# A gated linear-attention layer: value unit moved to the end of a head, steps at fixed places, two copies moved to ScalarE

## The chip, the cores and the metric

The kernel runs on one core of one Trainium2 chip. The metric is the device time of one execution in microseconds (us). One profiled execution gives the trace; the runs that are timed without a profile give the median.

## The reference, cut to what matters

One layer over 512 latent and 256 context tokens of width 2048. Two groups work on the same normalised input: a gated recurrence (RG-LRU, called A here) and a linear attention with a decay per key channel (HGRN2, called B here), 16 heads of 128 channels, run in both directions. The change touches B alone:

```
f = lb + (1 - lb) * sigmoid(f_pre);  k = 1 - f;  q = silu(q_pre)      # for each direction
S_t = diag(f_t) S_{t-1} + k_t v_t^T;  o_t = q_t S_t                   # 16 heads, chunked, forward and backward
y  = rmsnorm(o_fwd + o_bwd) * silu(g);  x = x + gate * (concat(y_A, y_B) @ w_out);  out = rmsnorm(x)
```

`gate` comes from `silu(c) @ ada_w`, a vector product that the kernel sums on VectorE ("gate sums").

## The kernel before, in words

**Tiling.** The projection is a list of units. A unit is 128 output columns of w_in: 16 blocks of 128 rows, in four groups g = 0..3 of four blocks k. Each block is three matmuls (the weights are split into a high and a low part, `whi` and `wlo`, and so is the input). A unit that needs only latent tokens (q, gb) has matmuls of 512 columns; one that needs all tokens (ff, fb, v) has pairs of 256 and 512 columns. Before each group, `p_conv` makes one `whi` (a cast on ScalarE) and one `wlo` (a subtraction on GpSimd) for a group four ahead, and `p_dma` fetches a weight tile on SP's queue six ahead. When a unit's last group is through, `evac_b` takes the unit's result out of PSUM.

**A head of B** is five units: q, gb (output gate), ff and fb (decay gates forward and backward) and v. From `ff` and `fb`, `evac_b` makes T (the decay f) and KK (k = 1 - f) with a sigmoid on ScalarE and two operations on VectorE. Then come the steps of the head, all of whose matmuls are put between the projection's matmuls on TensorE, in program order:

- `prep`: kd = k forward + k backward, the two halves of QQ = q * f (VectorE), and Kc, a copy of k (ScalarE);
- `level(0)` to `level(6)`: 16 (or 8) small score matmuls, then KK, QQ and T are multiplied or paired up for the next level (VectorE); level 0 begins with the diagonal `diag`, which needs kd, and then needs Kc and both halves of QQ; level 5 copies blocks of `mc` into `mg`;
- `ktr` x4 and, for v, x4: transposes of KK and v on VectorE, 16 instructions each;
- `umm` x3: state matmuls from the two transposed tiles; `omm`: 12 output matmuls of 128 x 128, then on ScalarE four squares, a table load and a square root, on VectorE a reciprocal and four scalings; `otr`: 16 transposes on VectorE; `fin`: one product (`ys`) and its store on GpSimd's queue.

**Order of the steps before.** A queue `wq`. After every second block TensorE's program comes to a place where `run_steps(1)` may take a step from the queue's head: at k = 3 always, at k = 1 only if the step is marked `fast` (transposes). The units of a head stand in the order q, gb, ff, v, fb, so the steps of a head are queued when its fb is out, and run beside the next head's units.

**Gate sums before.** In heads 1 to 13, at g = 2 of every unit, `gate_step` adds one weight tile (fetched by `gate_raw` in the unit before, from the same ring of six tiles as the weights) to `gacc` with one VectorE instruction.

**Engines are in order.** Each engine runs its instructions in program order; one that waits holds all behind it.

**Where a place stands.** 40 places to a head, two to a group. In the changed kernel place n of head h is reached after the n-th pair of blocks counted from the head's q. In a q or gb unit a place is six matmuls of 512 columns, in the others six pairs.

Of the kernel before, what the change touches and what calls it, by code (L numbers as in the profile page):

```python
# [8 lines left out]
F32 = mybir.dt.float32  # L9
F32R = mybir.dt.float32r  # L10
U8 = mybir.dt.uint8
AF = mybir.ActivationFunctionType
# [23 lines left out]
START = [0, 16, 1, 17, 18]  # L36
NS = len(START)
ORDER_A = [2] + [cb for h in range(3, NH) for cb in (16 + h, h)]
ORDER_B = [32 + g * 16 + h for h in range(NH) for g in (0, 4, 1, 3, 2)]


def view(t, off, dims):
# [9 lines left out]
def layer_kernel(ctx: ExitStack, tc, xT, xres, w0, wi, adas, adag, adagb, wo, par, lw, fw, cst, masks, out):  # L52
# [449 lines left out]
    evac_ga(2, PG[2])  # L502
    wq.append(lb1)

    gst = {}

    def gate_raw(i):
# [4 lines left out]
    def gate_step(i):  # L512
        q, kb = divmod(i, KB)
        if q >= 4:
            return
        if kb == 0:
            gst["acc"] = bw.tile([128, 512], F32, name="gacc", bufs=2)
        a = gst["acc"]
        t = wlin(gst.pop(("raw", i)))
        if kb == 0:  # L520
            dve.tensor_scalar(a, t, sc[:, 0:1], None, op0=ALU.mult)
        else:
            dve.scalar_tensor_tensor(a, t, sc[:, kb:kb + 1], a, op0=ALU.mult, op1=ALU.add)
        gate_raw(i + 1)
        if kb == KB - 1:
            def go():
                b = bq.tile([1, 512], F32, name="sg")
                sp.dma_start(b, adagb[q:q + 1, :])
                ph = psw.tile([128, 512], F32, name="w")
                pe.matmul(ph, ones, a, start=True, stop=True)  # L530
                o = ystage.tile([1, 512], F32, name="ys")
                dve.tensor_add(o, ph[0:1, :], b)
                pool.dma_start(gate_d[q:q + 1, :], o)
            wq.insert(1, go)

    bw = None
    bst = {}
# [2 lines left out]
        act.activation(dst[:, 0:C], ph[:, 0, 0:C], AF.Sigmoid)  # L540
        act.activation(dst[:, C:TA], ph[:, 1, :], AF.Sigmoid)

    def fast(f):
        f.fast = True
        return f

    def transpose(dst, src, ks):
        for i in ks:
            for j in range(4):
                dve.transpose(dst[32 * j:32 * j + 32, :, 32 * i:32 * i + 32], src[32 * i:32 * i + 32, :, 32 * j:32 * j + 32])  # L550

    def evac_b(h, kind, ph):
        s = bst.setdefault(h, {})
        if kind in ("q", "gb"):
            sg = bq.tile([128, T], F32, name="sg")
            act.activation(sg, ph[:, 1, :], AF.Sigmoid)
            t = bq.tile([128, T], F32, name=kind, bufs=2)
            dve.tensor_mul(t, ph[:, 1, :], sg)
            s[kind] = t
        elif kind == "v":  # L560
            t = bw.tile([128, TA], F32, name="ktok")
            act.copy(t[:, 0:C], ph[:, 0, 0:C])
            act.copy(t[:, C:TA], ph[:, 1, :])  # L563
            vt = bw.tile([128, 6, 128], F32, name="vtok", bufs=2)
            s["v"] = vt

            for i in range(4):
                wq.append(fast(lambda i=i: transpose(vt, t.rearrange("p (a b) -> p a b", b=128), (i,))))
        else:
            d = 0 if kind == "ff" else 1  # L570
            if d == 0:
                s["T"] = bw.tile([128, 2, TA], F32, name="T0")
                s["K"] = bw.tile([128, 2, TA], F32, name="KK")
            f, k = s["T"][:, d, :], s["K"][:, d, :]
            sig2(f, ph)
            i = 16 * d + h
            dve.tensor_scalar(f, f, lbt[:, 1, i:i + 1], lbt[:, 0, i:i + 1], op0=ALU.mult, op1=ALU.add)
            dve.tensor_scalar(k, f, -1.0, 1.0, op0=ALU.mult, op1=ALU.add)
            if d == 1:
                wq.extend(steps_b(h))  # L580

    def steps_b(h):
        s = bst[h]
# [32 lines left out]
        def level(l):  # L616
            def go():
                m = 1 << l
                if l == 0:
                    diag()  # L620
                K, Q, Tm = s["K"], s["Q"], s["T"]
                pw = psw.tile([128, 512], F32, name="w")
                if l < 5:
                    tiles32(pw, lambda c, j: s["Kc"][:, c, 32 * j:32 * j + 32],
                            lambda c, j: view(Q, 128 * c + 32 * j, [[2 * m, 16 // m], [T + m, 2], [1, m]]))
                elif l == 5:
                    tiles32(pw, lambda c, j: K[:, j % 2, C + 128 * c + 32 * j:C + 128 * c + 32 * j + 32],
                            lambda c, j: Q[:, 1 - j % 2, 128 * c + 32 * (j ^ 1):128 * c + 32 * (j ^ 1) + 32])
                else:
                    for c in range(4):  # L630
                        for j in range(2):
                            k0, q0 = C + 128 * c + 64 * j, 128 * c + 64 * (1 - j)
                            pe.matmul(pw[64 * j:64 * j + 64, 64 * c:64 * c + 64], K[:, j, k0:k0 + 64],  # L633
                                      Q[:, 1 - j, q0:q0 + 64], start=True, stop=True)
                nb = TA // m
                kk = view(K, 0, [[2 * m, nb // 2], [TA + m, 2], [1, m]])
                dve.tensor_mul(kk, kk, view(Tm, 1, [[2, nb // 2], [nb - 1, 2], [0, m]]))  # L637
                if l < 4:
                    kc_copy(2 * m)
                qq = view(Q, 0, [[2 * m, C // m], [T + m, 2], [1, m]])  # L640
                dve.tensor_mul(qq, qq, view(Tm, nb + 1 + C // m, [[2, C // m], [-nb - 1, 2], [0, m]]))  # L641
                T2 = bw.tile([128, 2, nb // 2], F32, name=f"T{l + 1}")
                dve.tensor_mul(T2.rearrange("p a b -> p (a b)"), view(Tm, 0, [[2, nb]]), view(Tm, 1, [[2, nb]]))  # L643
                s["T"] = T2
                if l < 5:
                    dve.copy_predicated(s["mc"], MK[:, l, None, :].to_broadcast([128, 4, 32]),
                                        pw[:, 0:128].rearrange("p (a b) -> p a b", b=32))
                elif l == 5:
                    mg = bw.tile([128, 4, 128], F32, name="mg")
                    s["mg"] = mg  # L650
                    for j in range(4):
                        r = slice(32 * j, 32 * j + 32)
                        i = j ^ 1
                        act.copy(mg[r, :, 32 * i:32 * i + 32], pw[r, 0:128].rearrange("p (a b) -> p a b", b=32))
                        dve.tensor_copy(mg[r, :, r], s["mc"][r])  # L655
                else:
                    p4 = pw[:, 0:256].rearrange("p (a b) -> p a b", b=64)
                    act.copy(s["mg"][0:64, :, 64:128], p4[0:64])
                    dve.tensor_copy(s["mg"][64:128, :, 0:64], p4[64:128])
            return go  # L660
# [53 lines left out]
            pool.dma_start(y_d[KB + h], y)  # L714
            del bst[h]

        return ([prep] + [level(l) for l in range(7)] + [fast(ktr(i)) for i in range(4)] + [umm(0), umm(4), umm(8), omm, otr, fin])

    def run_steps(n):
        for _ in range(n):  # L720
# [28 lines left out]
    for i in range(NP):  # L749
# [21 lines left out]
        for k in range(4):  # L771
            mm_unit(ph if full else ph[:, 1, :], hi[:, k, :], lo[:, k, :], 4 * g + k, full)
            if k % 2 == 0:
                continue
            if grp == "A":
                credit += 1.5 if full else 1.0
                while credit >= 1.33:
                    credit -= 1.33
                    run_steps(1)
            elif u < NA + 3:  # L780
                left = 2 * (4 * NA + 10 - i) + (k == 1)
                run_steps(max(1, -(-len(wq) // max(1, left))))
            elif k == 3 or (wq and hasattr(wq[0], "fast")):
                run_steps(1)
        if grp == "A":
            if g == 3:
                if cb >= 16:
                    evac_ga(cb - 16, ph[:, 1, :])
                else:
                    evac_xa(cb, ph[:, 0, 0:C], ph[:, 1, :])  # L790
                    push_a(cb)
        elif u >= NA + 5 and g == 2 and gi < 4 * KB:
            if gi == 0:
                gate_raw(0)
            gate_step(gi)
            gi += 1
        elif g == 3:
            evac_b(cb % 16, kind, ph)

    hctx.close()  # L800
# [39 lines left out]
    for q in range(4):  # L840
# [13 lines left out]
        for kb in range(2 * KB):  # L854
# [3 lines left out]
            if q == 0:  # L858
                y_conv(kb + 2)
                y_dma(kb + 4)  # L860
                if wq:
                    run_steps(1)
                elif op is None:
                    rctx.close()
                    qctx.close()
                    rctx = ExitStack()
                    yp2 = rctx.enter_context(tc.tile_pool(name="yp2", bufs=1, side="right"))
                    op = rctx.enter_context(tc.tile_pool(name="op", bufs=1, side="right"))
                    ssq = op.tile([128, 4, 4], F32, name="ssq")
# [85 lines left out]
```

## Time and profile before

| what | value |
|---|---|
| median of 3 runs (lowest, highest) | 2327.13 us (2324.47, 2329.04) |
| the profiled execution's own time | 2325.76 us |
| its span, first to last instruction | 2323.9 us |
| TensorE matmul busy | 2241.1 us (96%) |
| VectorE, GpSimd, ScalarE busy | 1424.9 (61%), 934.7 (40%), 883.8 us (38%) |
| mean granted TensorE clock | 0.996 of full speed |

Busy time of TensorE counts matmuls whose ends are modelled, so a short wait behind a matmul shows a little shorter in it than from start to start.

### The profile page before, as it was taken

To read this page: it belongs to the slowest core of one execution; us is meant where nothing else is said; L and a number is where in the kernel's file an instruction comes from. 1 tells how busy PE (TensorE), PEld (TensorE's weight loads), DVE (VectorE), ACT (ScalarE), POOL (GpSimd) and SP (SyncE) were. 2 spreads that over 40 slices of the span, in tenths; PEclk is the share of its full clock that TensorE was granted. 3 is DMA by queue.
4 is the path that set the end of the run, shared out by engine and by line. 5 is a ranking of instruction groups with operands and counts; after the bars stand their busy time and mean duration, and the time that the engine had idled before them with its cause. 6 is when DMAs were issued, how large, how long until landed. Compare 5 with 4: busy or idle time off the path is not lost.

```text
span 2323.9 us, 38899 instructions
## 1 busy us (share of the span) xinstructions
PE 2241.1 (96%) x15520; PEld 1867.6 (80%) x15520; DVE 1424.9 (61%) x2223; ACT 883.8 (38%) x1605; POOL 934.7 (40%) x682
## 2 busy tenths in 40 slices
PE   5999999999999999999999999999999998999998
PEld 3778888888888788888888878878878887788886
DVE  5557666666667766775786786686676577710011
ACT  4247776777622232232232223223223233332222
POOL 1235555565533333433343333333333233355552
PEclk9999999999999999999999999999999999999999
DMA  8952222222222222222222222222222123553433
GB/s 323 345 188 78 82 82 82 82 91 78 74 78 82 82 84 83 81 92 73 74 94 79 76 90 83 73 91 78 87 79 76 61 65 114 159 173 96 126 122 109
DMA packets 119086, 241.95 MB, mean 104 GB/s; under 512 B 13556, under 2 KB 13940, under 8 KB 118904
## 3 DMA queue, kind: packets, MB, share of 16 engines
q1 hardware_dynamic: 116216, 231.06, 30.1%
q0 software_dynamic: 2688, 8.40, 0.9%
q8 instruction: 122, 2.00, 0.3%
q14 instruction: 60, 0.49, 0.1%
HBM read 226.81 MB, written 12.59 MB: 103 GB/s over the span
## 4 chain that ended last, share of the span: by engine, by line
PE 65%; DVE 21%; issue 5%; ACT 5%; DMA 2%; POOL 2%; SPq 0%; ACTq 0%; POOLq 0%; DVEq 0%
PE m L180 23%; PE m L179 12%; PE w L850 8%; PE m L182 8%; PE m L850 6%; DVE ktok L550 5%; DVE KK L637 4%; DVE QQ L641 3%; PE w L678 2%; PE w L372 2%; DVE T L643 1%; DMA araw<-in_adas 1%; PE w L182 1%; POOL i L385 1%; DVE mg L655 1%
## 5 line engine op out<-in xcount | busy, mean ns | idle before, releaser
L128 POOL TENSOR_TENSOR wlo<-wraw,whi 128x512 fp32r<-128x512 f32 x556 | 786.5, 1419 | 1123.5 <-ACT whi L127 1054.6
L180 PE MATMUL m<-h,whi 128*128 128x512 f32 x1984 | 737.5, 394 | 0.0
L179 PE MATMUL m<-h,whi 128*128 128x256 f32 x1984 | 562.9, 284 | 1.4 <-ACT xp L323 1.4
L127 ACT CAST whi<-wraw 128x512 fp32r<-128x512 f32 x556 | 342.5, 620 | 548.8 <-PE m L180 181.0
L182 PE MATMUL m<-h,whi 128*128 128x512 f32 x1440 | 455.9, 398 | 0.0
L180 PEld LDWEIGHTS m<-h,whi 128*128 128x128 f32 x1984 | 372.0, 188 | 81.6 <-issue 0.7
L180 PE MATMUL m<-h,wlo 128*128 128x512 f32 x992 | 390.4, 394 | 0.0
L179 PEld LDWEIGHTS m<-h,whi 128*128 128x128 f32 x1984 | 374.7, 189 | 4.2 <-ACT xp L323 1.9
L182 PEld LDWEIGHTS m<-h,whi 128*128 128x128 f32 x1440 | 263.4, 188 | 54.8 <-issue 0.5
L182 PE MATMUL m<-h,wlo 128*128 128x512 f32 x720 | 281.2, 391 | 0.0
L179 PE MATMUL m<-h,wlo 128*128 128x256 f32 x992 | 278.9, 281 | 0.0
L180 PEld LDWEIGHTS m<-h,wlo 128*128 128x128 f32 x992 | 185.9, 187 | 44.6
L179 PEld LDWEIGHTS m<-h,wlo 128*128 128x128 f32 x992 | 187.4, 189 | 0.0
L637 DVE TENSOR_TENSOR KK<-KK,T 128x768 f32<-128x768 f32 x112 | 176.5, 1576 | 3.0 <-PE w L633 1.8
L182 PEld LDWEIGHTS m<-h,wlo 128*128 128x128 f32 x720 | 135.2, 188 | 29.6
L340 DVE SCALAR_TENSOR_TENSOR u<-xp,P,u 128x256 f32<-128x256 f32 x96 | 88.1, 978 | 104.1 <-ACT u L338 104.1
L550 DVE STREAM_TRANSPOSE ktok<-KK 32x384 f32<-32x384 f32 x256 | 145.7, 569 | 3.3
L587 ACT COPY Kc<-KK 128x512 f32<-128x512 f32 x80 | 54.7, 684 | 176.1 <-DVE KK L637 120.0
L641 DVE TENSOR_TENSOR QQ<-QQ,T 128x512 f32<-128x512 f32 x112 | 115.5, 1031 | 0.4
L550 DVE STREAM_TRANSPOSE vtok<-ktok 32x192 f32<-32x192 f32 x256 | 94.6, 369 | 13.2 <-ACT ktok L563 10.0
L850 PE MATMUL m<-whi,yh 128*128 128x512 f32 x256 | 102.1, 399 | 0.0
L850 PE MATMUL m<-wlo,yh 128*128 128x512 f32 x256 | 101.2, 395 | 0.0
(209 smaller groups left out, 3075.9 us busy)
## 6 DMA issues: line engine op xcount, KB each, us to landing
wraw<-in_wi SPq DMA_DIRECT2D x428, 256.0 KB, 3.1
araw<-in_adas SPq DMA_DIRECT2D x64, 512.0 KB, 8.8
wraw<-in_wo SPq DMA_DIRECT2D x128, 256.0 KB, 2.6
wraw<-in_adag SPq DMA_DIRECT2D x64, 256.0 KB, 2.6
y_d<-ys POOLq DMA_DIRECT2D x32, 256.0 KB, 2.4
wraw<-y_d SPq DMA_DIRECT2D x32, 256.0 KB, 2.8
h<-in_xT SPq DMA_DIRECT2D x16, 384.0 KB, 7.6
w0raw<-in_w SPq DMA_DIRECT2D x16, 320.0 KB, 9.6
```

The lines of the kernel that those rows point to most:

```text
L127: act.copy(hi, t)
L128: pool.tensor_sub(lo, t, hi.bitcast(F32))
L179: pe.matmul(ph[:, 0, 0:C], w, h[:, 0:C], start=s, stop=e)
L180: pe.matmul(ph[:, 1, :], w, h[:, C:TA], start=s, stop=e)
L182: pe.matmul(ph, w, h[:, C:TA], start=s, stop=e)
L340: dve.scalar_tensor_tensor(dst, xp[:, o + k:o + k + n], cw, dst, op0=ALU.mult, op1=ALU.add)
L372: pe.matmul(pl, w[:, i, :], x[:, C:TA], start=n == 0, stop=n == 2)
L550: dve.transpose(dst[32 * j:32 * j + 32, :, 32 * i:32 * i + 32], src[32 * i:32 * i + 32, :, 32 * j:32 * j + 32])
L587: act.copy(kc.rearrange("p c n -> p (c n)").rearrange("p (a b c) -> p a b c", b=2, c=m), view(s["K"], C, [[2 * m, C // m], [TA + m, 2], [1 ...
L637: dve.tensor_mul(kk, kk, view(Tm, 1, [[2, nb // 2], [nb - 1, 2], [0, m]]))
L641: dve.tensor_mul(qq, qq, view(Tm, nb + 1 + C // m, [[2, C // m], [-nb - 1, 2], [0, m]]))
L850: pe.matmul(pos[tk], y[:, 128 * tk:128 * tk + 128], wlin(x), start=(kb == 0 and n == 0), stop=(kb == 2 * KB - 1 and n == 2))
```

## The change

The units of a head now stand as q, gb, ff, fb, v. The queue for B's steps is gone: every step has a fixed place, counted from its own head's q: prep 33, levels 34, 37, 39, 42, 45, 48, 51, the KK transposes 52, 54, 56, 57, those of v 58 to 61, umm 62, 64, 66, omm 68, otr 69, fin 71 (places from 40 on lie beside the next head; places after 56 of the last head are spread by 1.9). k = 1 - f is an ACTIVATE (Identity) on ScalarE, and so are level 5's four copies of `mc`. v's staging tile has its own buffer. The five gate tiles of a head are fetched after ff's last group, fb's first three and v's first, and each is added one group later.

```diff
-ORDER_B = [32 + g * 16 + h for h in range(NH) for g in (0, 4, 1, 3, 2)]
+ORDER_B = [32 + g * 16 + h for h in range(NH) for g in (0, 4, 1, 2, 3)]
...
+    def at(slot, f):
+        sched.setdefault(slot, []).append(f)
...
-        gate_raw(i + 1)
...
-            wq.insert(1, go)
+            at(slot_now + 5, go)
...
+    PREP, LEVEL = 33, (34, 37, 39, 42, 45, 48, 51)
+    KTR, VTR, UMM, OMM, OTR, FIN = (52, 54, 56, 57), (58, 59, 60, 61), (62, 64, 66), 68, 69, 71
+    GATES = {("ff", 3), ("fb", 0), ("fb", 1), ("fb", 2), ("v", 0)}
+    def put(h, slot, f):
+        s = 2 * 20 * h + slot
+        if h == NH - 1 and slot > 56:
+            s += (slot - 56) * 9 // 10
+        at(s, f)
...
-            t = bw.tile([128, TA], F32, name="ktok")
+            t = bw.tile([128, TA], F32, name="vraw")
...
-            dve.tensor_scalar(k, f, -1.0, 1.0, op0=ALU.mult, op1=ALU.add)
+            act.activation(k, f, AF.Identity, scale=-1.0, bias=ones[:, 0:1])
...
-                        dve.tensor_copy(mg[r, :, r], s["mc"][r])
+                        act.copy(mg[r, :, r], s["mc"][r])
...
-            elif k == 3 or (wq and hasattr(wq[0], "fast")):
-                run_steps(1)
+            run_slot(slot_now)
...
-        elif u >= NA + 5 and g == 2 and gi < 4 * KB:
-            if gi == 0:
-                gate_raw(0)
+        if ("raw", gi) in gst:
             gate_step(gi)
             gi += 1
-        elif g == 3:
+        if u >= NA + 5 and (kind, g) in GATES:
+            gate_raw(gi)
+        if g == 3:
             evac_b(cb % 16, kind, ph)
```

In the output projection that follows the units, each weight block kb now runs the two places that are its own, before its matmuls.

VectorE's program before, from one head's `omm` (the reciprocal) to the next head's `prep` (kd and the two QQ), in the middle of B:

```order
L701 RECIPROCAL ss<-ss 128x4
L703 TENSOR_SCALAR kd<-w,ss 128x128 x4
L550 STREAM_TRANSPOSE mg<-kd 32x4x32 x16
L523 SCALAR_TENSOR_TENSOR gacc<-wraw,sc,gacc 128x512
L712 SCALAR_TENSOR_TENSOR ys<-mg,P,gb 128x512
L550 STREAM_TRANSPOSE vtok<-ktok 32x6x32 x16
L523 SCALAR_TENSOR_TENSOR gacc<-wraw,sc,gacc 128x512
L577 TENSOR_SCALAR T_7457<-T_7457,lbt 128x768
L578 TENSOR_SCALAR KK<-T_7457 128x768
L595 TENSOR_TENSOR kd<-KK 128x512
L598 TENSOR_TENSOR QQ<-q,T_7457 128x512
L599 TENSOR_TENSOR QQ<-q,T_7457 128x512
```

The same stretch of VectorE's program in the changed kernel:

```order
L713 RECIPROCAL ss<-ss 128x4
L715 TENSOR_SCALAR kd<-w,ss 128x128 x4
L551 STREAM_TRANSPOSE mg<-kd 32x4x32 x16
L529 SCALAR_TENSOR_TENSOR gacc<-wraw,sc,gacc 128x512
L724 SCALAR_TENSOR_TENSOR ys<-mg,P,gb 128x512
L529 SCALAR_TENSOR_TENSOR gacc<-wraw,sc,gacc 128x512
L589 TENSOR_SCALAR T_7439<-T_7439,lbt 128x768
L607 TENSOR_TENSOR kd<-KK 128x512
L610 TENSOR_TENSOR QQ<-q,T_7439 128x512
L611 TENSOR_TENSOR QQ<-q,T_7439 128x512
```

The transposes of v and the making of KK have left the stretch; two `gacc` are still in it.

ScalarE's program before, from the sigmoid of fb (T) to the copy of the diagonal (`mc`), same place:

```order
L540 ACTIVATE T_8294<-m 128x256
L541 ACTIVATE T_8294<-m 128x512
L127 CAST whi<-wraw 128x512
L587 COPY Kc<-KK 128x512
L127 CAST whi<-wraw 128x512
L613 COPY mc<-w 128x128
```

And in the changed kernel:

```order
L545 ACTIVATE T_9113<-m 128x256
L546 ACTIVATE T_9113<-m 128x512
L590 ACTIVATE KK<-T_9113,ones 128x768
L127 CAST whi<-wraw 128x512
L599 COPY Kc<-KK 128x512
L127 CAST whi<-wraw 128x512
L625 COPY mc<-w 128x128
```

The making of KK now stands between the sigmoid and the first of the two casts.

## Rows read from the trace of the kernel before

**Rows 1.** Busy time in three stretches: window, length, then busy us (instructions) by engine, clock.

```profile
1096.90:1181.30 84.40, 82.28 (x670) 69.45 (x669) 60.53 (x107) 24.26 (x52) 28.82 (x21) 1.00 0.25 82
1772.90:1855.40 82.50, 81.98 (x670) 69.36 (x669) 55.71 (x102) 24.36 (x52) 28.59 (x21) 1.00 0.20 68
1936.00:2050.00 114.00, 104.02 (x683) 83.65 (x682) 78.68 (x115) 44.54 (x88) 42.56 (x33) 0.97 0.51 162
```

**Rows 2.** TensorE's waits, 690 to 1936 us: total us, times, longest.

```profile
PE w L678 <- DVE ktok L550: 14.7, 13, 1.3
PE w L605 <- DVE T L643: 6.0, 12, 0.5
PE w L605 <- ACT Kc L587: 4.7, 12, 0.4
```

**Rows 3.** TensorE's waits, 1936 to 2060 us.

```profile
PE w L678 <- DVE ktok L550: 3.3, 1, 3.3
...
PE w L605 <- DVE QQ L599: 1.9, 1, 1.9
PE w L605 <- DVE kd L595: 1.7, 1, 1.7
```

**Rows 4.** Timeline of TensorE (start, us): diag and level 0 of a head; behind its omm.

```profile
1102.85 0.46 PE L605 MATMUL w<-q,kd 128*32 128x32 f32 x32
1103.13 0.56 PE L605 MATMUL w<-QQ,Kc 128*32 128x32 f32 x32
...
1156.57 0.36 PE L179 MATMUL m<-h,whi 128*128 128x256 f32 x1
```

**Rows 5.** Chain of waits, 1094 to 1100 us: a pair's first matmul, eight pairs apart.

```profile
1093.98 0.12 PE m L179
...
1096.75 0.12 PE m L179
```

**Rows 6.** Timeline of VectorE, after that omm.

```profile
1161.09 5.05 DVE L550 STREAM_TRANSPOSE mg<-kd 32x128 f32<-32x128 f32 x16
1166.17 0.75 DVE L523 SCALAR_TENSOR_TENSOR gacc<-wraw,sc,gacc 128x512 f32<-128x512 f32 x1
1166.84 0.74 DVE L712 SCALAR_TENSOR_TENSOR ys<-mg,P,gb 128x512 f32<-128x512 f32 x1
1167.50 6.11 DVE L550 STREAM_TRANSPOSE vtok<-ktok 32x192 f32<-32x192 f32 x16
```

**Rows 7.** Timeline of VectorE: fb's evacuation and prep.

```profile
1098.39 0.68 DVE L577 TENSOR_SCALAR T<-T,lbt 128x768 f32<-128x768 f32 x1 [8.34 <-ACT T L541]
1099.10 1.54 DVE L578 TENSOR_SCALAR KK<-T 128x768 f32<-128x768 f32 x1
1100.68 0.69 DVE L595 TENSOR_TENSOR kd<-KK 128x512 f32<-128x512 f32 x1
1101.29 0.69 DVE L598 TENSOR_TENSOR QQ<-q,T 128x512 f32<-128x512 f32 x1
```

**Rows 8.** Timeline of ScalarE, same place.

```profile
1100.68 0.87 ACT L587 COPY Kc<-KK 128x512 f32<-128x512 f32 x1 [1.82 <-DVE KK L578]
1101.45 0.61 ACT L127 CAST whi<-wraw 128x512 fp32r<-128x512 f32 x1
```

**Rows 9.** Groups by line and form, ScalarE, whole span: busy us, mean ns.

```profile
L389 ACT ACTIVATE r<-r,s 128x768 f32<-128x768 f32 x32 | 28.3, 930 | 0.2
L393 ACT ACTIVATE s<-s 128x768 f32<-128x768 f32 x32 | 25.3, 838 | 0.2
```

**Rows 10.** Timeline of VectorE, 1117 to 1122 us.

```profile
1117.75 0.95 DVE L637 TENSOR_TENSOR KK<-KK,T 128x768 f32<-128x768 f32 x1
1118.62 1.78 DVE L641 TENSOR_TENSOR QQ<-QQ,T 128x512 f32<-128x512 f32 x1
1120.32 1.29 DVE L643 TENSOR_TENSOR T<-T 128x48 f32<-128x48 f32 x1
```

**Rows 11.** Timeline of GpSimd, same stretch.

```profile
1118.18 3.36 POOL L128 TENSOR_TENSOR wlo<-wraw,whi 128x512 fp32r<-128x512 f32 x2 [2.14 <-PE w L605]
```

More of the change, by code (lines that the diff above doesn't have):

```diff
@@ L503, in layer_kernel @@
     wq.append(lb1)
+    sched = {}
+    slot_now = 0
+    def at(slot, f):
+        sched.setdefault(slot, []).append(f)
     gst = {}
@@ L541, in sig2 @@
         act.activation(dst[:, C:TA], ph[:, 1, :], AF.Sigmoid)
-    def fast(f):
-        f.fast = True
-        return f
     def transpose(dst, src, ks):
@@ L565, in evac_b @@
             s["v"] = vt
-            for i in range(4):
-                wq.append(fast(lambda i=i: transpose(vt, t.rearrange("p (a b) -> p a b", b=128), (i,))))
+            for i, at_ in enumerate(VTR):
+                put(h, at_, lambda i=i: transpose(vt, t.rearrange("p (a b) -> p a b", b=128), (i,)))
         else:
@@ L577, in evac_b @@
             dve.tensor_scalar(f, f, lbt[:, 1, i:i + 1], lbt[:, 0, i:i + 1], op0=ALU.mult, op1=ALU.add)
-            dve.tensor_scalar(k, f, -1.0, 1.0, op0=ALU.mult, op1=ALU.add)
+            act.activation(k, f, AF.Identity, scale=-1.0, bias=ones[:, 0:1])
             if d == 1:
-                wq.extend(steps_b(h))
+                steps_b(h)
     def steps_b(h):
@@ L715, in fin, with run_slot @@
             del bst[h]
-        return ([prep] + [level(l) for l in range(7)] + [fast(ktr(i)) for i in range(4)] + [umm(0), umm(4), umm(8), omm, otr, fin])
+        put(h, PREP, prep)
+        for l, at_ in enumerate(LEVEL):
+            put(h, at_, level(l))
+        for i, at_ in enumerate(KTR):
+            put(h, at_, ktr(i))
+        for i, at_ in enumerate(UMM):
+            put(h, at_, umm(4 * i))
+        put(h, OMM, omm)
+        put(h, OTR, otr)
+        put(h, FIN, fin)
+    def run_slot(n):
+        for f in sched.pop(n, ()):
+            f()
     def run_steps(n):
@@ L779, in layer_kernel @@
                     run_steps(1)
-            elif u < NA + 3:
+                continue
+            slot_now = 2 * (i - 4 * NA) + (k == 3)
+            if u < NA + 3:
                 left = 2 * (4 * NA + 10 - i) + (k == 1)
                 run_steps(max(1, -(-len(wq) // max(1, left))))
-            elif k == 3 or (wq and hasattr(wq[0], "fast")):
-                run_steps(1)
+            run_slot(slot_now)
         if grp == "A":
@@ L791, in layer_kernel @@
                     push_a(cb)
-        elif u >= NA + 5 and g == 2 and gi < 4 * KB:
-            if gi == 0:
-                gate_raw(0)
+            continue
+        if ("raw", gi) in gst:
             gate_step(gi)
             gi += 1
-        elif g == 3:
+        if u >= NA + 5 and (kind, g) in GATES:
+            gate_raw(gi)
+        if g == 3:
             evac_b(cb % 16, kind, ph)
@@ L860, in layer_kernel @@
                 y_dma(kb + 4)
-                if wq:
-                    run_steps(1)
-                elif op is None:
+                slot_now = 2 * (NP - 4 * NA + kb)
+                run_slot(slot_now)
+                run_slot(slot_now + 1)
+                if not sched and op is None:
                     rctx.close()
```

## The prediction, made before the changed kernel had run

> **What bounds the kernel now.** I read the busy shares of the engines first (the table above): TensorE has work for 96% of the span, VectorE for 61%. A change to VectorE's and ScalarE's order can therefore win only the moments in which TensorE stands still, and lose by making new ones. So the next view is the busy time of single stretches [rows 1]. The first stretch is one head of B in steady state, with gate sums: 84.40 us long, TensorE busy 82.28, so 2.1 us idle. The second is a head without gate sums: 82.50 us, 0.5 us idle. What TensorE has to do in a head is thus 82.50 - 0.5 = 82.0 us, and this change alters no matmul. The third stretch is the last head's steps, which run beside the output projection: 114.00 - 104.02 = 10.0 us idle. With 13 heads of the first kind, two of the second and the end, all that there is to win in B is 13 x 2.1 + 2 x 0.5 + 10.0 = 38.3 us.
>
> The view of TensorE's waits says for what it stands still. In the heads it is umm, for the transposes of KK (14.7 us over 13 heads), and the first score matmuls of a level, for T or Kc [rows 2]. At the end it is umm again (3.3), and there also diag for kd (1.7) and level 0 for QQ (1.9) [rows 3]. So in the heads prep is no problem now: in the timeline level 0 starts 0.28 us after diag, without a wait [rows 4].
>
> **What the change removes.** In the old order umm(0) stands 20 places after prep, now 29: seven more places of pairs and two shorter ones. A pair takes (1096.75 - 1093.98)/8 = 0.346 us [rows 5], a place of six 2.08, so VectorE has over 14.5 us more until umm needs the transposes. Against that v's transposes (6.11 us, [rows 6]) now come in between. More than 8 us of room against 1.3 us that it is late now at most [rows 2]: I count the umm waits as gone. Levels 1 to 6 stand two or three places apart instead of two short ones, with one gate sum between them instead of two; their waits I count as gone too. The making of KK on VectorE (1.54 us, [rows 7]) and the copies of mc move to ScalarE, which is busy 24 of 84 us in a head [rows 1]; the copies are needed only at omm, so they cost nothing. The gate tiles come in a bunch on SP's queue, but each is fetched a whole group (12 pairs, 4.2 us) before its sum, and VectorE gets to two of the sums only after 5 us of transposes: nothing, and if a tile is late, T below is late by as much.
>
> **What it adds: prep comes too early.** Prep was four places behind fb's evacuation with v's transposes and no omm just before it. Now omm stands three places before fb's end and diag three places behind it. I work out a head from the moment at which TensorE goes on after omm (1156.57, [rows 4]); call it 0.
>
> - TensorE: 6 places x 6 pairs x 0.346 = 12.5. Then diag is due, and level 0 at 12.5 + 0.28 = 12.8.
> - VectorE: omm's square root, scalings and otr's transposes stay as they are. The first gate sum behind them starts at 1166.17 - 1156.57 = 9.6 [rows 6]. From it to ys is 0.67, from ys to the next 0.66; the order now has a second gate sum (0.67) and then T of fb. T starts at 11.6, though fb's sums have lain in PSUM since 3 x 2.08 = 6.2. It is queued behind otr.
> - T takes 0.68, and the next starts 0.03 later [rows 7]: 12.3. KK is now an ACTIVATE of 128 x 768 with a scale and a bias. The trace has no such one; the nearest rows of that size take 0.93 (exponential with a scale) and 0.84 [rows 9]. I take 0.93, with either end moving the sum by 0.1 a head: 13.25.
> - kd (0.69) needs KK: 13.3 to 14.0. **Diag waits from 12.5 to 14.0: 1.5 us.**
> - The two QQ start 0.61 apart behind kd [rows 7]: undisturbed, the second ends at 15.2, when level 0, due at 14.0 + 0.28 = 14.3, would have waited 0.9. Kc (0.87, [rows 8]) is no later.
>
> They will not be undisturbed. ScalarE's next instruction behind KK is a cast of whi, then Kc, then another cast. Both casts have all they need by then, because ScalarE stood behind T for five us. Each lets GpSimd start a wlo: the first at about 13.25 + 0.6 = 13.85, while kd runs, the second 1.5 us later (0.87 + 0.61, [rows 8]), while the first QQ runs. What that does is in the trace: GpSimd starts two wlo back to back at 1118.18 [rows 11]; the KK that runs then ends undisturbed, the QQ behind it takes 1.78 instead of 0.69, and the T of 48 columns behind that takes 1.29 [rows 10]. They take turns, and each turn costs VectorE 1.1 us. Two turns put the end of the second QQ at 15.2 + 2.2 = 17.4. **Level 0 waits from 14.3 to 17.4: 3.1 us.** Together 4.6 us a head.
>
> **The sum.** Heads 1 to 13: 82.0 + 4.6 = 86.6 instead of 84.4, so 13 x 2.2 = +28.6. Heads 14 and 15 have no gate sums: all is 1.34 earlier, diag waits 0.1 and level 0 until 16.05 instead of 12.9, 3.3 in all against 0.5: 2 x 2.8 = +5.6. Head 0 has no omm before it; no wait. The end: its prep is counted already; umm has room; levels 4 and 6 still follow one weight block after the level before. I leave 3 us of the 10.0 (bounds 0 and 10): -7. Sum +27.2: 2325.8 (the profiled execution's own time) + 27.2 = 2353.0. The median of the runs shown is 1.4 above that execution; I stay at 2353.
>
> **Rivals.**
>
> - *One turn instead of two* (the second cast late by half a microsecond, so that its wlo finds the second QQ already running): 3.5 us a head, 13 x (82.0 + 3.5 - 84.4) = 14.3, the two heads 2 x (2.2 - 0.5) = 3.4, end -7: +10.7, 2336. For it: the second cast comes only 0.6 us before it would be too late. Chance 0.15.
> - *Not slower: no turn at all.* If GpSimd starts only after the second QQ has begun (14.5), because the cast waits for a weight tile or for TensorE, a head waits 1.5 + 0.9 = 2.4, as much as the umm and level waits that go: 13 x 0, 2 x (1.1 - 0.5), end -7: -5.8, 2320. Against it: casts run four groups ahead and nothing in rows 2 waits for weights. Chance 0.14.
> - *VectorE's load was what mattered, and all waits go*: -38.3, 2287.5. For it: the head without gate sums has shed 1.6 us of idle time for 4.8 us less VectorE work [rows 1]. Against it: T stands behind otr whatever VectorE's load is. Chance 0.05. The Trainium skill (Perfetto Trace Analysis, Optimizing Scalar/DVE Operations) says that work which either of the two can do may be offloaded to ScalarE where VectorE is saturated; by it this rival would be the forecast. The stretches here show VectorE busy for 61 of 84 us, which is not saturated.
> - *Worse*: a further wait of 1 us a head (umm's room is used up by wlo turns, or a gate tile is late before T): 2353 + 14 = 2367. Chance 0.06.
>
> **How the numbers follow.** My own case has 0.60; alone it reaches from 2344 to 2360 (ScalarE's KK at either end, the end of the kernel at 0 or 10 us, a fifth of the turns not met). The range over all reaches down to the no-turn case and up past the own case: 2320 to 2362. A measurement of this kernel can tell about 0.2%, 4.7 us. Faster by more: the all-gone case and most of the no-turn case, 0.16. Within: the rest of it and the low edge of one turn, 0.10. Slower: 0.74.
>
> **What would show it.** Right: TensorE's waits name diag for kd (about 1.4 a head) and level 0 for the second QQ (about 3), and no longer umm for the transposes; a head is 86 to 87 us long; between the sigmoid of fb and its T VectorE finishes otr; the two QQ behind kd take 1.7 to 1.8 us each beside a wlo. Wrong: T of fb starting less than 11 us behind omm, QQ of 0.69 us there, or a head below 84 us. The step most open to error is the second turn, then the end of the kernel.

## The result, and the profile after

The median after is 2394.6 us (four runs, 2394.05 to 2394.98), before, on the same chip, 2326.15 (four runs, 2324.47 to 2329.04): a ratio of 1.0288, interval 1.0273 to 1.0302. The change costs 68 us. The direction was forecast; the time lies 42 us above the forecast and 33 above the range.

The page of the changed kernel, its span and busy shares:

```profile
span 2392.7 us, 38976 instructions
...
PE 2275.1 (95%) x15520; PEld 1901.4 (79%) x15520; DVE 1339.8 (56%) x2127; ACT 936.9 (39%) x1701; POOL 921.4 (39%) x682
```

VectorE has 85 us less to do than before, and the kernel is slower. TensorE is busy 34 us longer for the same matmuls, which is the first sign that they themselves ran slower: the profiled execution's mean granted clock is 0.975 against 0.996. TensorE's waits over the whole span (total us, times, longest):

```profile
PE w L617 <- DVE QQ L611: 42.4, 15, 3.0
...
PE w L617 <- DVE kd L607: 19.3, 12, 3.7
...
PE w L690 <- DVE vtok L551: 4.3, 1, 4.3
...
PE w L645 <- DVE T L655: 0.9, 1, 0.9
PE w L617 <- ACT Kc L599: 0.9, 1, 0.9
```

The names of [rows 2] are gone: umm waits no more in the heads (the one wait for vtok is the last head's), nor do levels 1 to 6. In their place stand level 0 for the second QQ, 15 times, and diag for kd. Here is where they come from, in VectorE's timeline (start, us) of one head, from the end of otr:

```profile
1101.79 5.05 DVE L551 STREAM_TRANSPOSE mg<-kd 32x128 f32<-32x128 f32 x16
1106.87 0.75 DVE L529 SCALAR_TENSOR_TENSOR gacc<-wraw,sc,gacc 128x512 f32<-128x512 f32 x1
1107.54 0.74 DVE L724 SCALAR_TENSOR_TENSOR ys<-mg,P,gb 128x512 f32<-128x512 f32 x1
1108.20 0.75 DVE L529 SCALAR_TENSOR_TENSOR gacc<-wraw,sc,gacc 128x512 f32<-128x512 f32 x1
1108.87 0.67 DVE L589 TENSOR_SCALAR T<-T,lbt 128x768 f32<-128x768 f32 x1
1110.55 0.69 DVE L607 TENSOR_TENSOR kd<-KK 128x512 f32<-128x512 f32 x1 [1.00 <-ACT KK L590]
1111.15 1.77 DVE L610 TENSOR_TENSOR QQ<-q,T 128x512 f32<-128x512 f32 x1
1112.85 1.75 DVE L611 TENSOR_TENSOR QQ<-q,T 128x512 f32<-128x512 f32 x1
```

ScalarE and then GpSimd over the same moments:

```profile
1109.58 0.94 ACT L590 ACTIVATE KK<-T,ones 128x768 f32<-128x768 f32 x1 [4.89 <-DVE T L589]
1110.42 0.60 ACT L127 CAST whi<-wraw 128x512 fp32r<-128x512 f32 x1
1110.93 0.85 ACT L599 COPY Kc<-KK 128x512 f32<-128x512 f32 x1
1111.68 0.61 ACT L127 CAST whi<-wraw 128x512 fp32r<-128x512 f32 x1
```

```profile
1111.11 2.94 POOL L128 TENSOR_TENSOR wlo<-wraw,whi 128x512 fp32r<-128x512 f32 x2 [1.97 <-ACT whi L127]
```

VectorE goes from otr straight through both gate sums to T without a gap, although fb's sums were long ready. Then ScalarE makes KK and runs the casts that stood behind it, each cast releases a wlo, and the two QQ take 1.77 and 1.75 us, where the QQ of [rows 7] took 0.69. And this is TensorE at the same place, with the first matmul behind omm ahead of it:

```profile
1097.28 0.36 PE L179 MATMUL m<-h,whi 128*128 128x256 f32 x1
...
1111.29 0.46 PE L617 MATMUL w<-q,kd 128*32 128x32 f32 x32 [1.27 <-DVE kd L607]
1114.74 0.66 PE L617 MATMUL w<-QQ,Kc 128*32 128x32 f32 x32 [2.99 <-DVE QQ L611]
1115.33 0.58 PE L179 MATMUL m<-h,whi 128*128 128x256 f32 x1
...
1116.14 0.41 PE L179 MATMUL m<-h,whi 128*128 128x256 f32 x1
...
1116.78 0.41 PE L179 MATMUL m<-h,wlo 128*128 128x256 f32 x1
...
1120.45 0.28 PE L179 MATMUL m<-h,wlo 128*128 128x256 f32 x1
...
1120.80 0.28 PE L179 MATMUL m<-h,whi 128*128 128x256 f32 x1
```

Between 1109.63, where the last projection matmul starts, and 1115.33 TensorE does only the two short score steps and waits 4.3 us in two parts. Behind that a pair of projection matmuls starts every 0.64 us (1116.14 to 1116.78 and so on), not every 0.35 (1120.45 to 1120.80, and [rows 5]). The clock of a whole head, and of two stretches of it, from the first wait on and from within the second (window, length, busy us and instructions by engine, clock, DMA share, GB/s):

```profile
1040.00:1128.80 88.80, 84.53 (x669) 71.71 (x668) 55.05 (x101) 27.61 (x58) 27.61 (x21) 0.96 0.25 78
1109.60:1113.30 3.70, 0.88 (x35) 0.45 (x33) 2.75 (x3) 2.85 (x5) 2.19 (x2) 1.00 0.49 161
1113.40:1120.20 6.80, 5.46 (x48) 4.75 (x49) 6.29 (x7) 1.78 (x3) 1.17 (x2) 0.50 0.26 89
```

Diag still runs at the full clock. Within level 0's wait TensorE falls to half of it, 1.2 GHz of 2.4, and it is back 4.9 us after the projection has gone on (1115.33 to 1120.2). [Rows 1] had 1.00 in a head. A head is 88.75 us long instead of 84.4, one with the store of a gate row 92.15.

### The profile page after: what moved, and what is told of

Read it like the earlier page. It is cut to its first block, busy times and chain, and to the rows that moved or that the text cites. A ratio compares the mean times of both kernels' runs of the same rounds, so it can differ in the third digit from the quotient of the medians.

```text
span 2392.7 us, 38976 instructions
## 1 busy us (share of the span) xinstructions
PE 2275.1 (95%) x15520; PEld 1901.4 (79%) x15520; DVE 1339.8 (56%) x2127; ACT 936.9 (39%) x1701; POOL 921.4 (39%) x682
## 4 chain that ended last, share of the span: by engine, by line
PE 78%; DVE 8%; issue 6%; ACT 5%; DMA 2%; POOL 1%; SPq 0%; ACTq 0%; DVEq 0%; POOLq 0%
PE m L180 23%; PE m L182 19%; PE m L179 12%; PE w L877 7%; PE m L877 6%; DVE mg L551 2%; PE w L617 2%; PE w L372 2%; PE w L690 2%; PE w L182 1%; DVE QQ L611 1%; DMA araw<-in_adas 1%; PE w L257 1%; PE w L371 1%; POOL i L385 1%
## 5 line engine op out<-in xcount | busy, mean ns | idle before, releaser
L128 POOL TENSOR_TENSOR wlo<-wraw,whi 128x512 fp32r<-128x512 f32 x556 | 773.1, 1393 | 1186.7 <-ACT whi L127 1100.9
L180 PE MATMUL m<-h,whi 128*128 128x512 f32 x1984 | 760.2, 405 | 0.0
L179 PE MATMUL m<-h,whi 128*128 128x256 f32 x1984 | 576.8, 291 | 1.4 <-ACT xp L323 1.4
L180 PEld LDWEIGHTS m<-h,whi 128*128 128x128 f32 x1984 | 384.6, 194 | 86.5 <-issue 0.7
L182 PE MATMUL m<-h,whi 128*128 128x512 f32 x1440 | 452.9, 396 | 0.0
L180 PE MATMUL m<-h,wlo 128*128 128x512 f32 x992 | 398.5, 402 | 0.0
L179 PEld LDWEIGHTS m<-h,whi 128*128 128x128 f32 x1984 | 386.5, 195 | 5.4 <-ACT xp L323 1.9
L182 PEld LDWEIGHTS m<-h,whi 128*128 128x128 f32 x1440 | 264.5, 188 | 54.7
L182 PE MATMUL m<-h,wlo 128*128 128x512 f32 x720 | 281.1, 390 | 0.0
L180 PEld LDWEIGHTS m<-h,wlo 128*128 128x128 f32 x992 | 190.2, 192 | 48.1
L179 PEld LDWEIGHTS m<-h,wlo 128*128 128x128 f32 x992 | 191.9, 193 | 0.0
L653 DVE TENSOR_TENSOR QQ<-QQ,T 128x512 f32<-128x512 f32 x112 | 101.6, 907 | 156.0 <-PE w L617 156.0
L649 DVE TENSOR_TENSOR KK<-KK,T 128x768 f32<-128x768 f32 x112 | 143.2, 1278 | 47.6 <-PE w L645 40.4
L182 PEld LDWEIGHTS m<-h,wlo 128*128 128x128 f32 x720 | 135.2, 188 | 29.1
L697 DVE SCALAR_TENSOR_TENSOR S<-S,T,w 128x128 f32<-128x128 f32 x128 | 44.5, 348 | 105.6 <-PE w L690 61.4
```

Of the source, the lines that this page charges most:

```text
L128: pool.tensor_sub(lo, t, hi.bitcast(F32))
L179: pe.matmul(ph[:, 0, 0:C], w, h[:, 0:C], start=s, stop=e)
L180: pe.matmul(ph[:, 1, :], w, h[:, C:TA], start=s, stop=e)
L182: pe.matmul(ph, w, h[:, C:TA], start=s, stop=e)
```

## The experiments

Each kernel is the changed one with the edit shown, unless it says otherwise, timed against the kernel before on the same chip (median there 2328.64, 2328.65 or 2327.67).

**Later: prep's scores moved three places.** The idea is that nothing is slow in itself and level 0 is only asked for too early. If so, putting level 0 at place 37, with the levels behind it drawn together, should take away both waits at once.

```
-    PREP, LEVEL = 33, (34, 37, 39, 42, 45, 48, 51)
+    PREP, LEVEL = 33, (37, 39, 42, 44, 46, 48, 51)
```

> The changed kernel with level 0 at place 37 instead of 34 (levels 37, 39, 42, 44, 46, 48, 51), nothing else. Theory A: the loss is that diag and level 0 come before VectorE has kd and QQ; the trace of the changed kernel has QQ ready 17.1 us behind omm, and place 37 comes at 18.7. Then both waits (1.44 + 3.18 us a head) go, and with them the 5 us at half clock behind them (2.1 us a head): 15 x 6.7 = -100, 2295. Theory B: the loss comes from what moved to ScalarE and from the gate sums, whatever place prep has: a head stays above 86 us, 2350 or more. Levels 2 to 5 now stand closer together; if VectorE is late there, up to 2 us a head come back, 2325.

Measured: 2294.69 us, ratio 0.9853 [0.9838, 0.9867]. The waits from 690 to 2100 us and the window of a head:

```profile
PE w L690 <- DVE vtok L551: 4.3, 1, 4.3
PE w L617 <- ACT Kc L599: 1.5, 2, 0.9
PE w L617 <- DVE QQ L611: 0.6, 1, 0.6
PE w L617 <- DVE QQ L653: 0.5, 1, 0.5
```

```profile
1091.16:1173.10 81.94, 81.94 (x672) 69.69 (x671) 53.78 (x102) 27.44 (x58) 28.16 (x21) 1.00 0.25 85
```

One line turns a loss of 2.9% into a gain of 1.5%. A head is 81.94 us, the floor of 82.0 that was read from [rows 1]. All else of the change is still in it, so the place of diag and level 0 is what the change loses by.

**Fill: TensorE kept busy in the waits.** Of the 4.35 us by which a head grew, which part is wait and which is clock? Here TensorE multiplies something that nobody reads, six matmuls of 512 columns ahead of diag and thirteen ahead of level 0; the steps and the other engines' work are as in the changed kernel.

```
+        def fill(n):
+            dp = psw.tile([128, 512], F32, name="w")
+            z = hh[0][0]
+            for _ in range(n):
+                pe.matmul(dp, z[:, 0:128], z[:, C:TA], start=True, stop=True)
...
+                    fill(6)
                     diag()
+                    fill(13)
```

> The changed kernel with matmuls of 128 x 512 whose result nobody reads: 6 ahead of diag and 13 between diag and level 0, 0.228 us each, so that TensorE works through both waits (1.37 of 1.44 us, 2.96 of 3.18). Theory A: the waits last as long as before, but the clock stays at its upper level behind them; a head takes 86.6 instead of 88.75 us, 15 x 2.1 - 4.3 (head 0, which has no wait) = -28, 2367. Rival: the slow pairs behind level 0 have another cause (a busy port, late weights); then the filling changes nothing or costs, 2395 to 2400.

Measured: 2374.07 us, ratio 1.0194 [1.0177, 1.0211]. More work for TensorE, and 20.5 us less time. A head:

```profile
1035.40:1121.90 86.50, 86.50 (x688) 73.07 (x687) 56.24 (x101) 27.63 (x58) 27.67 (x21) 1.00 0.24 80
```

The two QQ there still take 1.79 and 1.78 us, so VectorE is as late as before; only the clock stays up. From q to q a head is 86.56 us, which is 82.0 + 4.56, the two waits (1.4 + 3.2) to within 0.1, against 88.75 without the filling. So the clock costs 2.2 us a head. Of the 7 us above the expected 2367 the trace shows 5: four heads, of 91.20, 89.48 and twice 87.43 us, are together 9.3 over the common one, where the changed kernel has two such heads, 3.4 and 0.9 over; those with 91.20 and 92.15 are the same head, with the store of a gate row.

**Kkdve: k = 1 - f back on VectorE.** Are the turns of QQ made by KK on ScalarE, which holds the casts up until T is there?

```
-            act.activation(k, f, AF.Identity, scale=-1.0, bias=ones[:, 0:1])
+            dve.tensor_scalar(k, f, -1.0, 1.0, op0=ALU.mult, op1=ALU.add)
```

> The changed kernel with k = 1 - f back on VectorE, nothing else. Theory A: KK on VectorE takes 0.7 us where no wlo runs beside it, and the two casts of whi no longer stand behind it in ScalarE's queue, so the wlo come at another time and the QQ meet no turn or one: diag waits 1.25, level 0 0.9 to 2.0, together 2.2 to 3.3 instead of 4.6: 15 x -2.4 = -36 or 15 x -1.3 = -20, 2359 to 2375 if the clock still falls, 2327 to 2343 if a shorter wait leaves it up. Rival: VectorE is what is short, and giving it back 1.5 us a unit makes each head longer: over 2395.

Measured: 2368.94 us, ratio 1.0172 [1.0157, 1.0187]. VectorE in one head:

```profile
1097.35 2.02 DVE L589 TENSOR_SCALAR T<-T,lbt 128x768 f32<-128x768 f32 x1
1099.40 0.56 DVE L590 TENSOR_SCALAR KK<-T 128x768 f32<-128x768 f32 x1
...
1100.61 0.69 DVE L610 TENSOR_TENSOR QQ<-q,T 128x512 f32<-128x512 f32 x1
1101.21 0.69 DVE L611 TENSOR_TENSOR QQ<-q,T 128x512 f32<-128x512 f32 x1
```

Yes: the QQ are undisturbed. But a wlo that starts at 1097.65 now falls on T, which takes 2.02 us in place of 0.67, so diag waits for kd 2.4 us from start to start in a common head, and level 0 some 0.8. A turn was moved, another went, and 26 us came back. The waits are still there with KK on either engine.

**Gates: the gate sums away from T.** Two gate sums (1.34 us) stand ahead of T. Here the five tiles of a head are fetched earlier and summed beside q, gb and the first half of ff, so that no sum stands between omm and prep.

```
-    GATES = {("ff", 3), ("fb", 0), ("fb", 1), ("fb", 2), ("v", 0)}
+    GATES = {("q", 1), ("q", 3), ("gb", 1), ("gb", 3), ("ff", 0)}
```

> The changed kernel with the five gate tiles of a head fetched in the q, gb and first ff groups (summed one group later), so that no gate sum stands between omm and prep. Theory A: T of fb starts 1.34 us earlier, diag waits 0.1 instead of 1.44, level 0 still 3.2 because both wlo turns stay, the clock still falls: 13 x -1.3 = -17, 2377. Rival: the sums were the cause (before, heads with sums were 1.9 us longer): the heads lose all waits, 2300 to 2320.

Measured: 2383.46 us, ratio 1.0233 [1.0218, 1.0249]. TensorE's waits, first lines of the whole span:

```profile
PE w L617 <- DVE QQ L611: 44.1, 15, 3.0
...
PE w L690 <- DVE vtok L551: 21.2, 14, 4.3
```

Diag no longer waits, level 0 waits as long as ever (both QQ still take 1.77 and 1.75 us), and umm now waits for v's transposes: on VectorE three of the sums that left T stand among the transposes of KK and v. Together these waits are as long as in the changed kernel (44.1 + 21.2 = 65.3 us against 42.4 + 19.3 + 4.3 = 66.0), and still 11 us came back. TensorE's busy time is 8 us shorter (2267.1 against 2275.1) and the mean clock 0.986 instead of 0.975, so most of the gain is the clock: in most heads it is down for 3.4 us, where the changed kernel has 6.8. The sums' places matter, but they are not what makes level 0 late.

**Defer: the casts out of the way.** The turns alone: the casts of v's first two groups are held back until v's third group, so that none stands behind KK.

```
-        p_conv()
+        late = grp == "B" and cb // 16 == 5
+        if not (late and g < 2):
+            p_conv()
+        if late and g == 2:
+            p_conv()
+            p_conv()
```

> The changed kernel with the weight casts of v's first two groups put off to its third, so that no wlo runs beside kd and the two QQ; prep and levels stay at 33 and 34. Theory A: the two turns on the shared operand path go, the second QQ ends 2.2 us earlier, level 0 waits 0.9 instead of 3.18, diag 1.44 as before: 2.3 us a head. If the clock still falls behind it a head is 86.4 (15 x -2.3 = -35, 2360), if it stays up 84.3 (15 x -4.5 = -67, 2328). Rival: the QQ are long for another reason (their operands, q from another unit): they stay at 1.77 and 1.75, 2395.

Measured: 2344.86 us, ratio 1.0067 [1.0052, 1.0082]. VectorE, and TensorE's waits over the span:

```profile
1097.08 0.68 DVE L610 TENSOR_TENSOR QQ<-q,T 128x512 f32<-128x512 f32 x1
1097.68 0.68 DVE L611 TENSOR_TENSOR QQ<-q,T 128x512 f32<-128x512 f32 x1
```

```profile
PE w L617 <- DVE kd L607: 18.6, 12, 3.8
PE w L617 <- DVE QQ L611: 12.6, 15, 0.8
```

The turns are gone, 50 us with them. What is left is diag's wait and 0.8 for level 0, near the 2.4 us a head that the rival without turns had said. Of the thirteen heads with gate sums four are 84.0 to 84.4 us long, which is 82.0 and the waits; in six, of 85.5 to 85.9, the clock fell behind the same waits. The other three have a gate row and are 85.9 to 88.8, and the clock fell in two of them; its mean over this execution is 0.990. So the time lies between the two values that were expected.

**Before with the two moves alone.** The kernel before, with KK and the copies of mc on ScalarE and nothing else changed.

> The kernel before with only the two moves to ScalarE (k = 1 - f and level 5's four copies of mc), in the old order with its queue. Theory A: a move to ScalarE is worth what it takes out of the chain that is late. The chain from fb to umm loses the copies (1.9 us) and of KK some 0.6, but kd now waits for KK at ScalarE and the casts come behind it, so a wlo turn or two falls on the QQ: umm's 1.4 us a head go, level 0 waits up to 1 us: 13 x -0.5 to 13 x -1.5, 2308 to 2322. Rival (VectorE's load is what counts): every wait goes, 2290. Rival (the move itself is what made the change slow): 2340 or more.

Measured: 2339.0 us, ratio 1.0044 [1.0029, 1.0059]: slower, where I had expected a gain. In the old order, too, the turns appear. Its VectorE and GpSimd:

```profile
1105.66 1.79 DVE L598 TENSOR_TENSOR QQ<-q,T 128x512 f32<-128x512 f32 x1
1107.37 1.76 DVE L599 TENSOR_TENSOR QQ<-q,T 128x512 f32<-128x512 f32 x1
```

```profile
1105.61 2.98 POOL L128 TENSOR_TENSOR wlo<-wraw,whi 128x512 fp32r<-128x512 f32 x2 [5.62 <-ACT whi L127]
```

In [rows 7] KK stood on VectorE, 1.54 us, and the QQ behind it were undisturbed. With KK on ScalarE the casts wait behind it and release their wlo just as the QQ start. Level 0 waits for QQ in 15 heads, 15.8 us in all, and umm still waits. No run moves only one of the two; that KK is the one that costs is read from these rows.

**Later with both moves undone.** The complement: level 0 at place 37, KK and the copies of mc on VectorE.

> The kernel with level 0 at place 37, with k = 1 - f and the copies of mc back on VectorE. Theory A: with prep's steps out of TensorE's way VectorE has room (55 of 82 us busy), so the moves to ScalarE are worth nothing: 2294 to 2300, a head 82 to 82.4. Rival: VectorE is short once the heads are 82 us long; waits of 1 us a head at levels 2 to 5 or at umm come back: 2310 or more.

Measured: 2293.94 us, ratio 0.9851 [0.9835, 0.9868], the same as later within what the runs can tell; a head is 81.86 us. Where there is room ahead of level 0, the moves to ScalarE are worth nothing either way.

**Place 36: how much room is enough?** Level 0 two places later instead of three.

```
-    PREP, LEVEL = 33, (34, 37, 39, 42, 45, 48, 51)
+    PREP, LEVEL = 33, (36, 39, 42, 44, 46, 48, 51)
```

> The changed kernel with level 0 at place 36 (levels 36, 39, 42, 44, 46, 48, 51). Theory A in numbers: place 36 ends 8 x 2.08 = 16.6 us behind omm; kd has long been ready, so diag waits nothing; the second QQ is ready at 17.1 to 17.4, level 0 due at 17.0 waits 0.1 to 0.5. A wait that short leaves the clock up: a head 82.1 to 82.5, 15 x -6.4 = -96, 2296 to 2304. Rival: any wait of level 0 there lets the clock fall: 84.5 a head, 2330.

Measured: 2302.61 us, ratio 0.9895 [0.9878, 0.9911]. Level 0 waits 0.4 us from start to start in a common head, and the clock stays up: 82.28 us. One head is 87.08 us long, where a gate row's store comes first and level 0 waits 2.6; its window has a clock of 0.98:

```profile
1005.00:1088.00 83.00, 82.76 (x665) 70.22 (x664) 53.80 (x102) 27.54 (x58) 27.38 (x21) 0.98 0.26 82
```

**Grow: the gate row out of its own tile.** In the head of 92.15 us the finished gate row is written into a `ys` tile, and the next `ys` waits until that row is stored. VectorE of the changed kernel there:

```profile
1015.40 0.67 DVE L537 TENSOR_TENSOR ys<-w,sg 1x512 f32<-1x512 f32 x1
1018.67 0.75 DVE L724 SCALAR_TENSOR_TENSOR ys<-mg,P,gb 128x512 f32<-128x512 f32 x1 [2.60 <-DMA gate_d<-ys]
```

The edit sums into the tile of the bias instead and stores from there:

```
-                o = ystage.tile([1, 512], F32, name="ys")
-                dve.tensor_add(o, ph[0:1, :], b)
-                pool.dma_start(gate_d[q:q + 1, :], o)
+                dve.tensor_add(b, ph[0:1, :], b)
+                pool.dma_start(gate_d[q:q + 1, :], b)
```

> The changed kernel with the gate row summed into and stored from its own bias tile instead of the buffer that ys uses; nothing else. In the changed kernel one of the four heads with a gate row is 92.14 us long instead of 88.75, because ys waits for the row's store (2.6 us) ahead of T, another is 89.67. Theory A: that goes, -3.4 to -4: 2390 to 2391. Rival: it was the place of the row's matmul and sum, not the shared buffer: no change, 2394 to 2395.

Measured: 2388.66 us, ratio 1.0264 [1.0248, 1.0279], 5.9 us below the changed kernel's median. The head of 92.15 becomes 89.05, and the fourteen heads together are 3.9 us shorter.

**Tail: what is left at the end.** Later, with grow's edit, and the last head's steps at listed places beside the output projection in place of the fixed formula: umm at 70, 73 and 76 instead of 67, 71 and 75, omm and otr one place later:

```
-            s += (slot - 56) * 9 // 10
+            s = 40 * h + {57: 57, 58: 59, 59: 61, 60: 63, 61: 65, 62: 70, 64: 73, 66: 76, 68: 79, 69: 81, 71: 84}[slot]
```

> The kernel with level 0 at place 37, and two more edits: the last head's umm, omm, otr at 70, 73, 76, 79, 81 instead of 67, 71, 75, 78, 80 (beside the output projection, where TensorE waited 4.3 us for v's transposes), and the gate row is summed into and stored from its own bias tile, not from the buffer that ys needs. Expected: 4.3 us at umm go, of the four gate rows 1 us in all: 2289 to 2291 beside 2294.7. Rival: the wait only moves to the end of the last head's chain: no change.

Measured: 2288.64 us, ratio 0.9827 [0.9813, 0.9842], the fastest of all and ahead of both kernels. The waits in the heads and the end, from 690 to 2100 us:

```profile
PE w L616 <- ACT Kc L598: 1.5, 2, 0.9
PE w L616 <- DVE QQ L652: 0.5, 1, 0.5
PE w L644 <- DVE T L654: 0.3, 1, 0.3
```

The 4.3 us for vtok are gone. What the view still names in this stretch is 2.3 us in all.

## Why the direction was right and the size wrong

**What held.** T starts 11.6 us behind omm (1108.87 - 1097.28), as forecast, behind otr and two gate sums. KK on ScalarE takes 0.94 (taken: 0.93). Diag waits 1.4 from start to start and level 0 3.2 (1.5 and 3.1 were forecast). Two turns, of 1.1 us each, fall on the two QQ; [rows 10, 11] had shown what one costs, and defer shows that without them level 0 is late by 0.8. The Trainium skill (SBUF — State Buffer, SBUF: two separate sides) says that VectorE and GpSimd share one pair of ports as a lock which an instruction holds to its end, and that a VectorE operation with two SBUF inputs falls under it against a GpSimd operation that reads SBUF. The trace agrees: two wlo in 2.94 us, two QQ of 1.77 and 1.75 beside them, and 0.68 with the wlo away. The umm and level waits of [rows 2] went. The floor of a head, 82.0 us, is what later and later_dve run at.

**The step that failed: the sum had no term for TensorE's clock.** It counted a head as 82.0 + 4.6 us, waits and nothing else, as if the matmuls behind a wait ran as fast as those ahead of it. They don't: the granted clock is 0.50 for five us behind level 0, in every head with both waits. Fill takes that away alone and gets 86.56 us, the forecast 86.6; without it a head is 88.75. For the fourteen heads from the second to the fifteenth 2.15 us each are 30 us, nearly three quarters of the miss of 41.6. The row that shows it was among those read: the third of [rows 1] has 0.97 for the stretch with the waits of 1.7, 1.9 and 3.3 in [rows 3], where the heads have 1.00. It was read for its idle time only.

**A term that was left out: the gate rows.** They were counted as nothing. In one head a row's store holds the next ys up, and with it T and diag; that head is 3.4 us longer than the others, of which grow takes 3.1. Grow's median is 5.9 lower, of which its heads show 3.9.

**The account.** By the two profiled executions the kernel is 2394.98 - 2325.76 = 69.2 us slower. The fourteen heads from the second to the fifteenth take 1245.68 us instead of 1178.19: 67.5. Forecast for them were 13 x 2.2 + 2.8 = 31.4; the clock is 14 x 2.15 = 30.1, the two longer heads 3.4 and 0.9 (the second has a gate row as well, and stays with grow), which leaves 1.7. Of that, 1.5 is on the side of before: its fourteen heads were taken as 13 x 84.4 + 82.5 = 1179.7 us. Outside them 1.7 us remain, of which 2.4 already stand where B begins: there grow is 3.5 ahead of the changed kernel though only gate rows differ, so this is the start of A and its gate rows or the spread between executions, and the runs do not tell the two apart.

What is left, head 0 and all from the last head on, is -0.7, against 2.8 - 7 = -4.2 forecast: the end was sized 3.5 us too low. Beside level 0's wait of 3.0 TensorE still waits there 4.3 us at umm, whose wait was thought gone, and 0.9 each for T and Kc, 6.1 us where 3 were left; tail takes the 4.3 back. The clock adds nothing to the difference at the end, for the kernel before already had two stretches of 3.4 us at half clock there, behind its waits of [rows 3], and the changed kernel has two as well. Before, then after:

```profile
1946.50:1949.90 3.40, 3.40 (x10) 2.52 (x8) 2.69 (x4) 0.69 (x1) 0.00 (x0) 0.50 0.33 84
1987.40:1990.80 3.40, 2.81 (x11) 2.65 (x12) 1.53 (x4) 0.27 (x1) 0.00 (x0) 0.50 0.59 181
```

```profile
2000.90:2004.20 3.30, 3.30 (x41) 2.85 (x30) 3.25 (x4) 0.68 (x1) 0.00 (x0) 0.50 0.30 84
2058.90:2062.30 3.40, 3.02 (x11) 2.86 (x12) 1.53 (x4) 0.27 (x1) 0.00 (x0) 0.50 0.69 221
```

**The rivals.** One turn and no turn are ruled out by the QQ rows, though defer shows that the no-turn case was priced right only where the clock stays up. "All waits go" is ruled out for this change; later shows that it needed three places more. The worse case, 2367 for a further wait, was too low, and for another reason. **The moves to ScalarE.** The forecast gave the copies of mc no cost, and no run tests them alone. It saw that KK would hold up the casts and counted the two turns. What it did not ask is whether the moves were worth making: both together, in the old order, cost 0.44%, and where there is room they are worth nothing.

## What to carry to other kernels

When a step is given a fixed place, count back from it along every in-order queue that its inputs pass through, here omm's scalings, otr, two sums, T, KK and the two subtractions on GpSimd that the casts release: the place must lie behind the last of them, and three places were worth 100 us. A wait of TensorE can cost twice: here 4.6 us of waits brought 2.2 us of slower matmuls with them. So ask of each forecast wait what the clock does behind it, and look in the clock column of every stretch that already has such a wait. Moving work to an idle engine also moves what stands behind it in that engine's queue; look at what that releases, and onto whom.

## What the runs showed of the hardware

- In a common head of the changed kernel TensorE's granted clock fell to 0.50 within level 0's wait of 3.0 us, which follows a wait of 1.3 and a short score step, and came back about five us after TensorE had work again; the cost was 2.2 us a head (88.75 against 86.56). With level 0's wait of 3.0 alone (gates) it fell in 13 of 15 heads; behind 1.3 and 0.8 (defer) in 8 of the 12 heads that have both; behind 2.6 in the one such head of place36. Behind single waits of 1.3 (umm, kernel before), 1.0 (level 0, before_act) and 0.4 (place36) it did not fall. Useless matmuls in the waits kept it at 1.00, but for one head where diag waits 2.4 us beyond the filling, and made the kernel 20.5 us faster (fill).
- Two wlo queued on GpSimd met two QQ on VectorE, and both QQ were longer by 1.1 us. T, with one tensor read, was met as well: in kkdve it took 2.02 us in place of 0.67, and the wlo that starts 0.30 us after it the usual 1.29. In the last head of the kernel before a wlo starts 0.35 us after the first QQ, and there that QQ kept its 0.68 and only the second took 1.75. No run settles which engine goes first.
